# A top-2 routing kernel with uneven token tiles, a zero-filled output tile and a one-input mask

## The chip, the cores and the metric

The kernel runs on one core of one Trainium2 chip. The metric is the device time of one execution in microseconds (us). The kernel before took 14.62 us (median of 3 runs, 14.59 to 14.70). At this length a tenth of a microsecond is 0.7% of an execution.

## The reference

```python
router_logits = np.random.randn(16, 1024, 8).astype(np.float32)     # batch, seq, experts; k = 2

def reference(router_logits, k):
    logits_max = np.max(router_logits, axis=-1, keepdims=True)
    probs = np.exp(router_logits - logits_max)
    probs = probs / np.sum(probs, axis=-1, keepdims=True)
    return np.argsort(probs, axis=-1)[..., -k:]                      # int64: runner-up, winner
```

The softmax keeps the order of the logits, so the task is: for each of 16,384 tokens, the positions of the second largest and the largest of 8 numbers. The output is int64, so each answer is a 32-bit word followed by a zero word.

## The kernel before

The tokens lie on 128 partitions, 128 tokens each, and go through in two tiles of 64. All arithmetic is on VectorE. A first instruction, the pack, overwrites the lowest three bits of each logit with its expert number. Then a tournament of maxima and minima finds the two largest numbers, and the last instruction keeps only the lowest three bits of each.

```python
    andmask = const_pool.tile([P, 1], i32)
    nc.vector.memset(andmask, -8)
    mask4 = const_pool.tile([P, 4], i32)              # 7, 0, 7, 0
    nc.vector.memset(mask4[:, 0::2], 7)
    nc.vector.memset(mask4[:, 1::2], 0)
    for it in range(n_tiles):                         # two tiles of T = 64 tokens
        nc.sync.dma_start(out=x, in_=in_h[:, c0 : c0 + T, :])
        # the pack: x = (x & -8) | expert number, 8 words per token
        nc.vector.scalar_tensor_tensor(out=x_i, in0=x_i, scalar=andmask[:, 0:1], in1=iota_b,
                                       op0=Alu.bitwise_and, op1=Alu.bitwise_or)
        # A = max, Bm = min of experts 0-3 with 4-7 (4 words per token each)
        # T1 = max, UV[0:2] = min of A's halves; UV[2:4] = max of Bm's halves (2 each)
        nc.vector.tensor_reduce(out=FS[:, :, 1], in_=T1, axis=X, op=Alu.max)    # the winner
        nc.vector.tensor_reduce(out=U2, in_=T1, axis=X, op=Alu.min)
        nc.vector.tensor_reduce(out=W, in_=UV, axis=X, op=Alu.max)
        nc.vector.tensor_tensor(out=FS[:, :, 0], in0=U2, in1=W, op=Alu.max)     # the runner-up
        # the mask: 4 words per token, from FS with each word read twice, and 7, 0, 7, 0
        nc.vector.tensor_tensor(out=o_v, in0=fs_b, in1=m4_b, op=Alu.bitwise_and)
        nc.scalar.dma_start(out=out_h[:, c0 : c0 + T, :], in_=o)
```

(The tournament is told in comments.)

Of the kernel before, what the change touches and what calls it, by code (L numbers as in the profile page):

```python
# [1 line left out]

# [4 lines left out]

TOKENS_PER_TILE = 64
USE_POOL_L1 = False  # L10


@with_exitstack
def kernel(
    ctx: ExitStack,
    tc: tile.TileContext,
    router_logits: bass.AP,
    k: bass.AP,
    out: bass.AP,
):  # L20
    nc = tc.nc
    P = nc.NUM_PARTITIONS
    Alu = mybir.AluOpType

    assert isinstance(k, int) and k == 2, f"kernel specialized for k=2, got {k}"

    B, S, E = router_logits.shape
    n_tokens = B * S
    assert E == 8
    assert n_tokens % P == 0  # L30
    T_ALL = n_tokens // P

    fp32 = mybir.dt.float32
    i32 = mybir.dt.int32

    in_h = router_logits.tensor.reshape([P, T_ALL, E])
    out_h = out.tensor.reshape([P, T_ALL, 2]).bitcast(i32)

    const_pool = ctx.enter_context(tc.tile_pool(name="consts", bufs=1))
    x_pool = ctx.enter_context(tc.tile_pool(name="x", bufs=2))  # L40
    mid_pool = ctx.enter_context(tc.tile_pool(name="mid", bufs=2))
    out_pool = ctx.enter_context(tc.tile_pool(name="o", bufs=2))

    iota8 = const_pool.tile([P, E], i32)
    nc.gpsimd.iota(iota8, pattern=[[1, E]], base=0, channel_multiplier=0)  # L45

    andmask = const_pool.tile([P, 1], i32)
    nc.vector.memset(andmask, -8)  # L48

    mask4 = const_pool.tile([P, 4], i32)  # L50
    nc.vector.memset(mask4[:, 0::2], 7)  # L51
    nc.vector.memset(mask4[:, 1::2], 0)  # L52

    T = TOKENS_PER_TILE
    n_tiles = T_ALL // T

    for it in range(n_tiles):
        c0 = it * T

        x = x_pool.tile([P, T, E], fp32)  # L60
        nc.sync.dma_start(out=x, in_=in_h[:, c0 : c0 + T, :])

        x_i = x.bitcast(i32)
        iota_b = iota8[:, None, :].to_broadcast([P, T, E])

        nc.vector.scalar_tensor_tensor(  # L66
            out=x_i,
            in0=x_i,
            scalar=andmask[:, 0:1],
            in1=iota_b,  # L70
            op0=Alu.bitwise_and,
            op1=Alu.bitwise_or,
        )

        A = mid_pool.tile([P, T, 4], fp32)
        Bm = mid_pool.tile([P, T, 4], fp32)
        l1_eng = nc.gpsimd if USE_POOL_L1 else nc.vector
        l1_eng.tensor_tensor(out=A, in0=x[:, :, 0:4], in1=x[:, :, 4:8], op=Alu.max)  # L78
        l1_eng.tensor_tensor(out=Bm, in0=x[:, :, 0:4], in1=x[:, :, 4:8], op=Alu.min)  # L79

        T1 = mid_pool.tile([P, T, 2], fp32)
        UV = mid_pool.tile([P, T, 4], fp32)
        nc.vector.tensor_tensor(out=T1, in0=A[:, :, 0:2], in1=A[:, :, 2:4], op=Alu.max)  # L83
        nc.vector.tensor_tensor(  # L84
            out=UV[:, :, 0:2], in0=A[:, :, 0:2], in1=A[:, :, 2:4], op=Alu.min
        )
        nc.vector.tensor_tensor(  # L87
            out=UV[:, :, 2:4], in0=Bm[:, :, 0:2], in1=Bm[:, :, 2:4], op=Alu.max
        )

        FS = mid_pool.tile([P, T, 2], fp32)
        U2 = mid_pool.tile([P, T], fp32)
        W = mid_pool.tile([P, T], fp32)
        nc.vector.tensor_reduce(  # L94
            out=FS[:, :, 1], in_=T1, axis=mybir.AxisListType.X, op=Alu.max
        )
        nc.vector.tensor_reduce(out=U2, in_=T1, axis=mybir.AxisListType.X, op=Alu.min)  # L97
        nc.vector.tensor_reduce(out=W, in_=UV, axis=mybir.AxisListType.X, op=Alu.max)  # L98
        nc.vector.tensor_tensor(out=FS[:, :, 0], in0=U2, in1=W, op=Alu.max)  # L99

        o = out_pool.tile([P, T, 4], i32)
        o_v = o.rearrange("p t (c two) -> p t c two", two=2)
        fs_b = FS.bitcast(i32)[:, :, :, None].to_broadcast([P, T, 2, 2])
        m4_b = (
            mask4[:, None, 0:4]
            .rearrange("p t (c two) -> p t c two", two=2)
            .to_broadcast([P, T, 2, 2])
        )
        nc.vector.tensor_tensor(out=o_v, in0=fs_b, in1=m4_b, op=Alu.bitwise_and)  # L109

        nc.scalar.dma_start(out=out_h[:, c0 : c0 + T, :], in_=o)


# [1 line left out]
_INS = ['router_logits', 'k']  # L115
_OUTS = [((16, 1024, 2), 'int64')]
#: Inputs that are plain numbers.
_NUMBERS = {'k': 2}


# [26 lines left out]
```

## Time and profile before

| what | value |
|---|---|
| time | 14.62 us (profiled execution 14.69, span 12.9) |
| first input issued, first pack starts | 0.74, 3.75 us |
| VectorE from first pack to end of last mask | 6.59 us (3.75 to 10.34) |
| last store, issue to landing | about 1.8 us |

The first view is the profile's chain of waits: the work that ended last, followed backwards, as shares of the span by engine.

```profile
DVE 51%; DMA 22%; issue 1%; DVEq 0%
```

VectorE (DVE) alone makes up half of the span, the first input transfer another 22%. The rest is the start, before the chain begins, and the last store after the last VectorE instruction. Where that time lies is seen in the timeline. Its columns are: start and length in us, engine, line of the program, operation, output and inputs, shape; in brackets the idle time before and what ended it.

```profile
0.74 0.85 SPq L61 DMA_DIRECT2D x<-in_router_logits_dram  x2
...
3.75 1.41 DVE L66 SCALAR_TENSOR_TENSOR x<-x,andmask,iota 128x512 int32<-128x512 int32 x2 [2.82 <-DMA x<-in_router_logits_dram]
5.08 0.42 DVE L78 TENSOR_TENSOR A<-x 128x256 f32<-128x256 f32 x1
5.42 0.42 DVE L79 TENSOR_TENSOR Bm<-x 128x256 f32<-128x256 f32 x1
5.75 0.28 DVE L83 TENSOR_TENSOR T<-A 128x128 f32<-128x128 f32 x1
...
9.21 0.41 DVE L98 TENSOR_REDUCE W<-UV 128x64 f32<-128x256 f32 x1
9.65 0.23 DVE L99 TENSOR_TENSOR FS<-U,W 128x64 f32<-128x64 f32 x1
9.91 0.43 DVE L109 TENSOR_TENSOR o<-FS,mask 128x256 int32<-128x256 int32 x1
```

Two things are to be read here. Bm starts 0.34 us after A and T 0.33 us after Bm, although A and Bm last 0.42: neighbours overlap, and what an instruction costs is the step from its start to the next start, not its length. And where an instruction needs the result of its neighbour (W, FS and mask at the end) the overlap is lost: FS starts 0.44 us after W, not 0.33.

The DMA issues of the same page give the bytes of one transfer and the median time from issue to landing.

```profile
x<-in_router_logits_dram SPq DMA_DIRECT2D x2, 256.0 KB, 3.0
out_dram<-o ACTq DMA_DIRECT2D x2, 128.0 KB, 1.8
```

### The profile page before, as it was taken

The numbers are of one execution on the slowest core, as the hardware profiler recorded it, in microseconds if no ns is written. First come the engines' busy times: TensorE is split into PE (matmuls) and PEld (weight loads), VectorE is DVE, ScalarE is ACT, GpSimd is POOL, SyncE is SP. The second block draws the span as 40 slices with busy tenths as digits, with TensorE's granted clock in tenths as the row PEclk, the third lists the DMA queues.
The fourth block names the chain that finished last, engine by engine and source line by source line (L and its number), as shares of the span: only waits on it lengthen the run. The fifth ranks groups of instructions, "written<-read, shape, count | busy, mean of one in ns | idle before, by whom it ended". The sixth has DMA issues, their size and how long they took to land.

```text
span 12.9 us, 77 instructions
## 1 busy us (share of the span) xinstructions
DVE 6.6 (51%) x25; POOL 0.3 (3%) x5
## 2 busy tenths in 40 slices
DVE  0030000000039999999999999999988900000000
POOL 2340000000000000000000000000000000000000
DMA  0000048999520000000000000000380000190000
GB/s 0 0 0 0 0 57 222 286 343 406 222 89 0 0 0 0 0 0 0 0 0 0 0 0 0 0 0 0 130 273 3 0 0 0 60 330 16 0 0 0
DMA packets 576, 0.79 MB, mean 61 GB/s; under 512 B 64, under 2 KB 320, under 8 KB 576
## 3 DMA queue, kind: packets, MB, share of 16 engines
q1 hardware_dynamic: 288, 0.52, 12.7%
q10 hardware_dynamic: 288, 0.26, 6.1%
HBM read 0.52 MB, written 0.26 MB: 61 GB/s over the span
## 4 chain that ended last, share of the span: by engine, by line
DVE 51%; DMA 22%; issue 1%; DVEq 0%
DMA x<-in_router_logits_dram 22%; DVE x L66 11%; DVE o L109 6%; DVE Bm L79 5%; DVE A L78 5%; DVE W L98 5%; DVE UV L87 3%; DVE UV L84 3%; DVE T L83 3%; DVE FS L94 3%; DVE U L97 3%; DVE FS L99 3%; DVEq L66 0%
## 5 line engine op out<-in xcount | busy, mean ns | idle before, releaser
L66 DVE SCALAR_TENSOR_TENSOR x<-x,andmask,iota 128x512 int32<-128x512 int32 x2 | 1.4, 748 | 2.8 <-DMA x<-in_router_logits_dram 2.8
L109 DVE TENSOR_TENSOR o<-FS,mask 128x256 int32<-128x256 int32 x2 | 0.8, 422 | 0.0
L79 DVE TENSOR_TENSOR Bm<-x 128x256 f32<-128x256 f32 x2 | 0.8, 419 | 0.0
L78 DVE TENSOR_TENSOR A<-x 128x256 f32<-128x256 f32 x2 | 0.8, 417 | 0.0
L98 DVE TENSOR_REDUCE W<-UV 128x64 f32<-128x256 f32 x2 | 0.8, 408 | 0.0
L84 DVE TENSOR_TENSOR UV<-A 128x128 f32<-128x128 f32 x2 | 0.6, 286 | 0.0
L87 DVE TENSOR_TENSOR UV<-Bm 128x128 f32<-128x128 f32 x2 | 0.6, 286 | 0.0
L83 DVE TENSOR_TENSOR T<-A 128x128 f32<-128x128 f32 x2 | 0.6, 285 | 0.0
L94 DVE TENSOR_REDUCE FS<-T 128x64 f32<-128x128 f32 x2 | 0.6, 279 | 0.0
L97 DVE TENSOR_REDUCE U<-T 128x64 f32<-128x128 f32 x2 | 0.6, 276 | 0.0
L48 DVE MEMSET andmask<- 128x1 int32 x1 | 0.1, 59 | 0.8 <-PEq L128 0.8
L99 DVE TENSOR_TENSOR FS<-U,W 128x64 f32<-128x64 f32 x2 | 0.4, 222 | 0.0
L45 POOL IOTA iota<- 128x8 int32 x1 | 0.1, 135 | 0.4 <-PEq L142 0.4
L128 POOL MEMSET const-float32-0.0<- 128x1 f32 x1 | 0.1, 99 | 0.2 <-issue 0.2
L128 POOL MEMSET const-bfloat16-1.0<- 128x1 bf16 x1 | 0.1, 102 | 0.0
L128 POOL MEMSET const-uint8-127<- 128x1 uint8 x1 | 0.1, 102 | 0.0
L128 POOL MEMSET const-float32-1.0<- 128x1 f32 x1 | 0.1, 99 | 0.0
L51 DVE MEMSET mask<- 128x2 int32 x1 | 0.1, 60 | 0.0
L52 DVE MEMSET mask<- 128x2 int32 x1 | 0.1, 60 | 0.0
## 6 DMA issues: line engine op xcount, KB each, us to landing
x<-in_router_logits_dram SPq DMA_DIRECT2D x2, 256.0 KB, 3.0
out_dram<-o ACTq DMA_DIRECT2D x2, 128.0 KB, 1.8
```

The costliest lines, as they stand in the source:

```text
L66: nc.vector.scalar_tensor_tensor(out=x_i, in0=x_i, scalar=andmask[:, 0:1], in1=iota_b, op0=Alu.bitwise_and, op1=Alu.bitwise_or,)
L78: l1_eng.tensor_tensor(out=A, in0=x[:, :, 0:4], in1=x[:, :, 4:8], op=Alu.max)
L79: l1_eng.tensor_tensor(out=Bm, in0=x[:, :, 0:4], in1=x[:, :, 4:8], op=Alu.min)
L83: nc.vector.tensor_tensor(out=T1, in0=A[:, :, 0:2], in1=A[:, :, 2:4], op=Alu.max)
L84: nc.vector.tensor_tensor(out=UV[:, :, 0:2], in0=A[:, :, 0:2], in1=A[:, :, 2:4], op=Alu.min)
L87: nc.vector.tensor_tensor(out=UV[:, :, 2:4], in0=Bm[:, :, 0:2], in1=Bm[:, :, 2:4], op=Alu.max)
L94: nc.vector.tensor_reduce(out=FS[:, :, 1], in_=T1, axis=mybir.AxisListType.X, op=Alu.max)
L97: nc.vector.tensor_reduce(out=U2, in_=T1, axis=mybir.AxisListType.X, op=Alu.min)
L98: nc.vector.tensor_reduce(out=W, in_=UV, axis=mybir.AxisListType.X, op=Alu.max)
L99: nc.vector.tensor_tensor(out=FS[:, :, 0], in0=U2, in1=W, op=Alu.max)
L109: nc.vector.tensor_tensor(out=o_v, in0=fs_b, in1=m4_b, op=Alu.bitwise_and)
L128: nc = _bacc.Bacc("TRN2", target_bir_lowering=False, num_devices=1)
```

## The change

It wants VectorE to start sooner (a first tile of 32 tokens instead of 64), to keep the smaller tile's work ahead of the second tile's pack (an ordering edge between instructions, which is no wait on a semaphore), and to write half as many words at the end: the zero words are put there by memsets while VectorE waits for its first input, and the mask becomes an instruction with one tensor input. One small constant is also set on GpSimd instead of VectorE, before the first input lands.

```diff
-TOKENS_PER_TILE = 64
+CHUNKS = [32, 96]
...
-    nc.vector.memset(andmask, -8)
-    (mask4: 7, 0, 7, 0)
+    nc.gpsimd.memset(andmask, -8)
+    for it, T in enumerate(CHUNKS):
+        oz = out_pool.tile([P, T, 4], i32, name=f"o{it}", tag=f"o{it}")
+        nc.vector.memset(oz, 0)
+        o_tiles.append(oz)
...
+        if it > 0:
+            tc.add_manual_dep(pack.ins, w_prev.ins.name, ...NoSync...)   # pack behind W of the tile before
...
-        nc.vector.tensor_tensor(out=o_v, in0=fs_b, in1=m4_b, op=Alu.bitwise_and)
+        nc.vector.tensor_scalar(out=o[:, :, 0:4:2], in0=FS.bitcast(i32),
+                                scalar1=7, scalar2=None, op0=Alu.bitwise_and)
```

More of the change, by code (lines that the diff above doesn't have):

```diff
@@ L7 @@
 from concourse._compat import with_exitstack
-TOKENS_PER_TILE = 64
-USE_POOL_L1 = False
+CHUNKS = [32, 96]
+SPLIT_IN_DMA = False
+SPLIT_LAST_OUT = False
+ACT_ZERO_PACK = True
 @with_exitstack
@@ L31 @@
     T_ALL = n_tokens // P
+    assert sum(CHUNKS) == T_ALL
     fp32 = mybir.dt.float32
@@ L47 @@
     andmask = const_pool.tile([P, 1], i32)
-    nc.vector.memset(andmask, -8)
-    mask4 = const_pool.tile([P, 4], i32)
-    nc.vector.memset(mask4[:, 0::2], 7)
-    nc.vector.memset(mask4[:, 1::2], 0)
-    T = TOKENS_PER_TILE
-    n_tiles = T_ALL // T
-    for it in range(n_tiles):
-        c0 = it * T
-        x = x_pool.tile([P, T, E], fp32)
-        nc.sync.dma_start(out=x, in_=in_h[:, c0 : c0 + T, :])
+    nc.gpsimd.memset(andmask, -8)
+    if not ACT_ZERO_PACK:
+        mask4 = const_pool.tile([P, 4], i32)
+        nc.vector.memset(mask4[:, 0::2], 7)
+        nc.vector.memset(mask4[:, 1::2], 0)
+    n_chunks = len(CHUNKS)
+    o_tiles = []
+    for it, T in enumerate(CHUNKS):
+        oz = out_pool.tile([P, T, 4], i32, name=f"o{it}", tag=f"o{it}")
+        nc.vector.memset(oz, 0)
+        o_tiles.append(oz)
+    c0 = 0
+    for it, T in enumerate(CHUNKS):
+        last = it == n_chunks - 1
+        x = x_pool.tile([P, T, E], fp32, name=f"x{it}", tag=f"x{it}")
+        src = in_h[:, c0 : c0 + T, :]
+        if SPLIT_IN_DMA:
+            nc.sync.dma_start(out=x[0:64], in_=src[0:64])
+            nc.scalar.dma_start(out=x[64:128], in_=src[64:128])
+        else:
+            nc.sync.dma_start(out=x, in_=src)
         x_i = x.bitcast(i32)
         iota_b = iota8[:, None, :].to_broadcast([P, T, E])
-        nc.vector.scalar_tensor_tensor(
+        pack = nc.vector.scalar_tensor_tensor(
             out=x_i,
@@ L73 @@
         )
-        A = mid_pool.tile([P, T, 4], fp32)
-        Bm = mid_pool.tile([P, T, 4], fp32)
-        l1_eng = nc.gpsimd if USE_POOL_L1 else nc.vector
-        l1_eng.tensor_tensor(out=A, in0=x[:, :, 0:4], in1=x[:, :, 4:8], op=Alu.max)
-        l1_eng.tensor_tensor(out=Bm, in0=x[:, :, 0:4], in1=x[:, :, 4:8], op=Alu.min)
-        T1 = mid_pool.tile([P, T, 2], fp32)
-        UV = mid_pool.tile([P, T, 4], fp32)
+        if it > 0:
+            tc.add_manual_dep(
+                pack.ins, w_prev.ins.name,
+                mybir.DependencyInfo(
+                    mybir.DependencyClass.NoSync, mybir.DependencyReason.DATA
+                ),
+                reason="work of the chunk before first",
+            )
+        A = mid_pool.tile([P, T, 4], fp32, name=f"A{it}", tag=f"A{it}")
+        Bm = mid_pool.tile([P, T, 4], fp32, name=f"B{it}", tag=f"B{it}")
+        nc.vector.tensor_tensor(out=A, in0=x[:, :, 0:4], in1=x[:, :, 4:8], op=Alu.max)
+        nc.vector.tensor_tensor(out=Bm, in0=x[:, :, 0:4], in1=x[:, :, 4:8], op=Alu.min)
+        T1 = mid_pool.tile([P, T, 2], fp32, name=f"T1{it}", tag=f"T1{it}")
+        UV = mid_pool.tile([P, T, 4], fp32, name=f"UV{it}", tag=f"UV{it}")
         nc.vector.tensor_tensor(out=T1, in0=A[:, :, 0:2], in1=A[:, :, 2:4], op=Alu.max)
@@ L89 @@
         )
-        FS = mid_pool.tile([P, T, 2], fp32)
-        U2 = mid_pool.tile([P, T], fp32)
-        W = mid_pool.tile([P, T], fp32)
+        FS = mid_pool.tile([P, T, 2], fp32, name=f"FS{it}", tag=f"FS{it}")
+        U2 = mid_pool.tile([P, T], fp32, name=f"U2{it}", tag=f"U2{it}")
+        W = mid_pool.tile([P, T], fp32, name=f"W{it}", tag=f"W{it}")
         nc.vector.tensor_reduce(
@@ L97 @@
         nc.vector.tensor_reduce(out=U2, in_=T1, axis=mybir.AxisListType.X, op=Alu.min)
-        nc.vector.tensor_reduce(out=W, in_=UV, axis=mybir.AxisListType.X, op=Alu.max)
+        w_prev = nc.vector.tensor_reduce(out=W, in_=UV, axis=mybir.AxisListType.X, op=Alu.max)
         nc.vector.tensor_tensor(out=FS[:, :, 0], in0=U2, in1=W, op=Alu.max)
-        o = out_pool.tile([P, T, 4], i32)
-        o_v = o.rearrange("p t (c two) -> p t c two", two=2)
-        fs_b = FS.bitcast(i32)[:, :, :, None].to_broadcast([P, T, 2, 2])
-        m4_b = (
-            mask4[:, None, 0:4]
-            .rearrange("p t (c two) -> p t c two", two=2)
-            .to_broadcast([P, T, 2, 2])
-        )
-        nc.vector.tensor_tensor(out=o_v, in0=fs_b, in1=m4_b, op=Alu.bitwise_and)
-        nc.scalar.dma_start(out=out_h[:, c0 : c0 + T, :], in_=o)
+        o = o_tiles[it]
+        if ACT_ZERO_PACK:
+            nc.vector.tensor_scalar(
+                out=o[:, :, 0:4:2],
+                in0=FS.bitcast(i32),
+                scalar1=7,
+                scalar2=None,
+                op0=Alu.bitwise_and,
+            )
+        else:
+            o_v = o.rearrange("p t (c two) -> p t c two", two=2)
+            fs_b = FS.bitcast(i32)[:, :, :, None].to_broadcast([P, T, 2, 2])
+            m4_b = (
+                mask4[:, None, 0:4]
+                .rearrange("p t (c two) -> p t c two", two=2)
+                .to_broadcast([P, T, 2, 2])
+            )
+            nc.vector.tensor_tensor(out=o_v, in0=fs_b, in1=m4_b, op=Alu.bitwise_and)
+        dst = out_h[:, c0 : c0 + T, :]
+        if last and SPLIT_LAST_OUT:
+            nc.scalar.dma_start(out=dst[0:64], in_=o[0:64])
+            nc.sync.dma_start(out=dst[64:128], in_=o[64:128])
+        else:
+            nc.scalar.dma_start(out=dst, in_=o)
+        c0 += T
 _INS = ['router_logits', 'k']
```

## The prediction

> **What bounds the kernel now.** One chain, by the profile's chain of waits: the first input transfer (issued at 0.74 us, released the VectorE at 3.62), then VectorE alone from 3.75 to 10.34 us without a pause, then the last output transfer (issued 10.37, median 1.8 us to landing), then the end of the 12.9 us span. The second input is needed at 4.41 us and is there.
>
> **VectorE's cost per instruction.** From the timeline's start-to-start steps: tensor_tensor on 256 elements per partition 0.33 us, on 128 elements 0.20, on 64 elements 0.13. That is about 0.067 us plus 1.04 ns per element; the two-operation pack (512) steps 0.66, so about 0.13 us fixed. An instruction that needs the result of the one just before it loses another 0.11 to 0.13 us (W at 9.21, then FS at 9.65 instead of 9.54, then mask at 9.91 instead of 9.78).
>
> **What changes.**
> - First tile 32 tokens instead of 64: 128 KB instead of 256. The DMA queue shares give about 90 ns per input packet (2 KB) and 44 ns per output packet (1 KB); a 1 KB input packet I estimate at 50 to 60 ns. Eight packets per engine make it 0.3 us earlier (0.2 to 0.4): the pack starts near 3.45 us. On the critical path in full. The fixed part of the transfer, the larger, stays.
> - Output: the masking tensor_tensor writes 4 words per token; the tensor_scalar writes 2, the zero words come from memsets. That saves 256 elements, 0.27 us, all critical. If the op runs two elements per cycle, another 0.1 us. The Trainium skill, "VectorE: DVE Perf Modes", section "The perf-mode tier table", gives tensor_scalar on 4-byte SBUF data that double rate; no instruction of this trace shows it, so I count it half.
> - The memsets of both output tiles (128 and 384 elements, together at most about 0.7 us) run between 0.8 and 1.6 us, while VectorE waits for data: free.
> - The instruction count after the first landing stays 22.
> - The ordering edge puts the second pack behind W of the first chunk. So pack and A of the first chunk now stand next to each other: +0.11 us. I expect the second pack, then A, to fill the gaps around FS and mask of the first chunk, as A and Bm do now. The second pack starts near 5.2 us, when its input (near 4.3) has long landed.
> - Last store 192 KB instead of 128: 8 packets per engine, half as large again, +0.15 us.
>
> **Sum.** VectorE ends near 9.75 us instead of 10.34 (0.3 landing, 0.32 output, 0.11 back, rest rounding); minus 0.15 for the store: 0.42 us gained. Predicted 14.2 us (ratio 0.97), range 13.95 to 14.42. Chances: faster by over 2% 0.73, within 2% 0.26, slower 0.01.
>
> **What would show it.** First pack starting at 3.35 to 3.55 us; no wait for the second input; tensor_scalar 96 tokens lasting 0.25 us (double rate) or 0.35 (single); memsets over by 1.7 us; last mask ending 9.6 to 9.9; last store 1.9 to 2.0 us to landing.
>
> **What would make it wrong.** The first transfer lands hardly earlier, because its time is latency rather than bytes (then about 14.5, within 2%); the scheduler leaves FS and mask of the first chunk back to back and A right behind the pack (+0.35 us, no gain beyond 2%); strided writes of the tensor_scalar run slowly; or the store of 1.5 KB rows is quicker than I count, with a double-rate tensor_scalar (then 14.0).

## The result

The changed kernel took 14.09 us (median of 12 runs, 14.01 to 14.45), the kernel before in all its runs up to then 14.71 us (15 runs, 14.45 to 14.83). The ratio is 0.964 (95% interval 0.960 to 0.968): faster. Ratios here are the mean time of one kernel's fast runs over that of the other's in the same rounds, so they are not quite the ratio of the medians. On one core "fast" and "slow" only mean that a run lies within 1.5% of the fastest of its kernel or above that. Both profiled executions, 14.69 us before and 14.29 us after, were slow, so the two profiles compare slow with slow.

The timeline of the changed kernel, same columns:

```profile
0.73 0.84 SPq L74 DMA_DIRECT2D x<-in_router_logits_dram  x2
...
0.83 0.57 DVE L62 MEMSET o<- 128x128 int32 x2 [0.83 <-PEq L164]
...
3.45 0.48 DVE L79 SCALAR_TENSOR_TENSOR x<-x,andmask,iota 128x256 int32<-128x256 int32 x1 [2.05 <-DMA x<-in_router_logits_dram]
3.97 0.29 DVE L98 TENSOR_TENSOR A<-x 128x128 f32<-128x128 f32 x1
...
5.04 0.28 DVE L118 TENSOR_REDUCE W<-UV 128x32 f32<-128x128 f32 x1
5.23 1.01 DVE L79 SCALAR_TENSOR_TENSOR x<-x,andmask,iota 128x768 int32<-128x768 int32 x1
6.16 0.19 DVE L119 TENSOR_TENSOR FS<-U,W 128x32 f32<-128x32 f32 x1
6.28 0.56 DVE L98 TENSOR_TENSOR A<-x 128x384 f32<-128x384 f32 x1
6.75 0.19 DVE L123 TENSOR_SCALAR o<-FS 128x64 int32<-128x64 int32 x1
...
9.23 0.26 DVE L119 TENSOR_TENSOR FS<-U,W 128x96 f32<-128x96 f32 x1
9.52 0.26 DVE L123 TENSOR_SCALAR o<-FS 128x192 int32<-128x192 int32 x1
```

The first pack starts 0.30 us sooner. The memsets end at 1.40 us, two microseconds before they could hurt. The first tile's pack and A are now neighbours, and A waits for the pack's end. The second pack and A of the second tile fill the gaps around FS and mask of the first. The last mask lasts 0.26 us where it lasted 0.43. VectorE ends at 9.78 us, 0.56 us sooner, after a stretch of 6.33 us.

And its DMA issues:

```profile
x<-in_router_logits_dram SPq DMA_DIRECT2D x1, 384.0 KB, 3.1
out_dram<-o ACTq DMA_DIRECT2D x1, 192.0 KB, 1.9
x<-in_router_logits_dram SPq DMA_DIRECT2D x1, 128.0 KB, 2.6
out_dram<-o ACTq DMA_DIRECT2D x1, 64.0 KB, 1.6
```

The last store gives back part of it: 192 KB land 1.9 us after their issue, 128 KB took about 1.8. From the end of the last mask to the end of the execution it is 4.51 us, where it was 4.35. From profile to profile 0.40 us remain (14.69 to 14.29).

### The profile page after: what moved, and what is told of

Its sections match the earlier page's. It is cut to its first block, busy times and chain, and to the rows that moved or that the text cites. A ratio compares the mean times of both kernels' runs of the same rounds, so it can differ in the third digit from the quotient of the medians.

```text
span 12.5 us, 77 instructions
## 1 busy us (share of the span) xinstructions
DVE 6.8 (54%) x24; POOL 0.4 (3%) x6
## 4 chain that ended last, share of the span: by engine, by line
DVE 50%; DMA 21%; issue 2%; DVEq 0%
DMA x<-in_router_logits_dram 21%; DVE x L79 11%; DVE A L98 6%; DVE B L99 5%; DVE W L118 5%; DVE UV L104 3%; DVE T L103 3%; DVE UV L107 3%; DVE FS L114 3%; DVE U L117 3%; DVE o L123 3%; DVE FS L119 3%; DVEq L79 0%
## 5 line engine op out<-in xcount | busy, mean ns | idle before, releaser
L79 DVE SCALAR_TENSOR_TENSOR x<-x,andmask,iota 128x256 int32<-128x256 int32 (+1 forms) x2 | 1.5, 747 | 2.0 <-DMA x<-in_router_logits_dram 2.0
L62 DVE MEMSET o<- 128x128 int32 (+1 forms) x2 | 0.5, 272 | 0.9 <-PEq L164 0.8
L98 DVE TENSOR_TENSOR A<-x 128x128 f32<-128x128 f32 (+1 forms) x2 | 0.8, 424 | 0.0
L99 DVE TENSOR_TENSOR B<-x 128x128 f32<-128x128 f32 (+1 forms) x2 | 0.8, 416 | 0.0
L118 DVE TENSOR_REDUCE W<-UV 128x32 f32<-128x128 f32 (+1 forms) x2 | 0.8, 408 | 0.0
L104 DVE TENSOR_TENSOR UV<-A 128x64 f32<-128x64 f32 (+1 forms) x2 | 0.6, 285 | 0.0
L107 DVE TENSOR_TENSOR UV<-B 128x64 f32<-128x64 f32 (+1 forms) x2 | 0.6, 285 | 0.0
L103 DVE TENSOR_TENSOR T<-A 128x64 f32<-128x64 f32 (+1 forms) x2 | 0.6, 284 | 0.0
L114 DVE TENSOR_REDUCE FS<-T 128x32 f32<-128x64 f32 (+1 forms) x2 | 0.6, 278 | 0.0
L117 DVE TENSOR_REDUCE U<-T 128x32 f32<-128x64 f32 (+1 forms) x2 | 0.6, 276 | 0.0
```

What stands on the lines that cost most here:

```text
L62: nc.vector.memset(oz, 0)
L79: pack = nc.vector.scalar_tensor_tensor(out=x_i, in0=x_i, scalar=andmask[:, 0:1], in1=iota_b, op0=Alu.bitwise_and, op1=Alu.bitwise_or,)
L98: nc.vector.tensor_tensor(out=A, in0=x[:, :, 0:4], in1=x[:, :, 4:8], op=Alu.max)
L99: nc.vector.tensor_tensor(out=Bm, in0=x[:, :, 0:4], in1=x[:, :, 4:8], op=Alu.min)
L103: nc.vector.tensor_tensor(out=T1, in0=A[:, :, 0:2], in1=A[:, :, 2:4], op=Alu.max)
L104: nc.vector.tensor_tensor(out=UV[:, :, 0:2], in0=A[:, :, 0:2], in1=A[:, :, 2:4], op=Alu.min)
```

## The experiments

Theory: the gain comes from the output step; the early start is real but is paid back by the gap behind the first pack and by the larger last store. Rival: the early start carries the gain.

The executions of one kernel vary by some 0.3 us, which is as much as the parts to be told apart. All profiles show where that lies: in the start of the first pack. So each profiled execution is split into the start of the first pack and the rest (its time minus that start):

| kernel | profiled time | first pack starts | rest |
|---|---|---|---|
| before | 14.69 | 3.75 | 10.94 |
| before, again (e11) | 14.80 | 3.86 | 10.94 |
| changed | 14.29 | 3.45 | 10.84 |
| changed, again (e5) | 14.27 | 3.43 | 10.84 |
| changed, again (e12) | 14.21 | 3.37 | 10.84 |
| e1 output step only | 14.32 | 3.79 | 10.53 |
| e2 split and edge only | 14.40 | 3.16 | 11.24 |
| e3 changed, no edge | 14.71 | 3.46 | 11.25 |
| e4 changed, two-input mask | 14.16 | 3.19 | 10.97 |
| e6 changed, tiles 16 and 112 | 14.02 | 2.77 | 11.25 |
| e7 changed, last store split | 14.89 | 3.42 | 11.47 |
| e8, e10 losers | 13.47 | 3.18 | 10.29 |
| e9 losers, tiles 24 and 104 | 13.36 | 3.00 | 10.36 |

The rest repeats to 0.01 us in every kernel that was profiled more than once. Below, an execution is called late or early by this start: with a first transfer of 128 KB, late is near 3.45 us and early near 3.17. Within one kernel the profiled starts differ by 0.11 us at most, so it is not shown directly that the rest is the same early and late. What speaks for it: the time from the end of the last mask to the end of the execution is 4.50 to 4.52 us in every profile with a 192 KB store that is not split, early (e2, e4, e8, e10) or late (changed, e3, e5, e12). In e3 and e6 the rest also holds a wait for the second input, so there it depends on when the first pack started.

### e1: the output step on the even tiles

```diff
-CHUNKS = [32, 96]
+CHUNKS = [64, 64]
-        if it > 0:        # the ordering edge
+        if False:
```

> The new output step and zero memsets on the old even tiles (64 and 64 tokens), without the ordering edge. Ledger theory (the split earns 0.3 us at the start and pays 0.11 us for the gap between pack and A and 0.15 us for the larger last store, so it is nearly a wash, and the output step earns 0.35 us): the first pack starts at 3.75 us as before, the last mask ends near 9.97 us, the store lands 1.8 us after issue, and the time is within 0.1 us of the changed kernel, ratio to the kernel before about 0.97. Rival (the earlier start carries the gain): the time stays within 0.1 us of the kernel before.

Measured: 14.09 us (median of 7), ratio 0.963 (0.955 to 0.970), as fast as the whole change. The first pack and the last mask:

```profile
3.79 1.41 DVE L79 SCALAR_TENSOR_TENSOR x<-x,andmask,iota 128x512 int32<-128x512 int32 x2 [2.39 <-DMA x<-in_router_logits_dram]
...
9.75 0.23 DVE L123 TENSOR_SCALAR o<-FS 128x128 int32<-128x128 int32 x1
```

The first pack starts at 3.79 us, as before, and the rest falls from 10.94 to 10.53. The output step alone earns 0.41 us. That the early start alone carries the gain, the rival, is ruled out.

### e2: the split and the edge with the old mask

```diff
-ACT_ZERO_PACK = True
+ACT_ZERO_PACK = False      # tensor_tensor with mask4, 4 words per token
-        nc.vector.memset(oz, 0)
```

> The uneven split and the ordering edge with the old masking operation (four words per token, tile of constants, no zero memsets). Ledger theory: first pack at 3.45 us, last mask ends 0.35 to 0.4 us later than in the changed kernel (near 10.15 us), store 1.9 us, so the time is within 0.1 us of the kernel before, ratio 0.99 to 1.0. Rival (the earlier start carries the gain): ratio about 0.97 or below.

Measured: 14.48 us (6 runs), ratio 0.990 (0.985 to 0.996). The first pack and the last mask:

```profile
3.16 0.49 DVE L78 SCALAR_TENSOR_TENSOR x<-x,andmask,iota 128x256 int32<-128x256 int32 x1 [2.27 <-DMA x<-in_router_logits_dram]
...
9.34 0.56 DVE L137 TENSOR_TENSOR o<-FS,mask 128x384 int32<-128x384 int32 x1
```

The rest grows from 10.94 to 11.24 us: 0.15 us in VectorE's stretch (6.74 us) and the remainder behind it, in the larger store. Against that stands the earlier start, 0.30 us between executions that land late. Late against late, the two sum to nothing. All six runs of e2 were near 14.47 us and its profile starts the pack at 3.16 us; the split's 1% here comes with such early landings (more on them under "Why the prediction was right"), and in e11 one kernel against itself differs by as much. The parts add up: 10.94 - 0.41 + 0.30 = 10.83, and the changed kernel has 10.84.

### e3: the changed kernel without the edge

```diff
-        if it > 0:
+        if False:
```

> The changed kernel without the ordering edge: the compiled order then has the second pack right behind the first. Theory that the edge is needed by the split: the second pack waits for the second input until about 4.35 us, VectorE is idle some 0.45 us from 3.9 us on, and against that pack and A no longer wait for each other (0.11 us), so the kernel is about 0.35 us slower than the changed kernel and about as slow as the kernel before. Rival (the edge is an ornament): the same time as the changed kernel within 0.1 us.

Measured: 14.64 us (6 runs), ratio 0.994 (0.986 to 1.003): as slow as the kernel before. Its timeline shows why:

```profile
3.46 0.49 DVE L79 SCALAR_TENSOR_TENSOR x<-x,andmask,iota 128x256 int32<-128x256 int32 x1 [2.06 <-DMA x<-in_router_logits_dram]
4.40 1.02 DVE L79 SCALAR_TENSOR_TENSOR x<-x,andmask,iota 128x768 int32<-128x768 int32 x1 [0.46 <-DMA x<-in_router_logits_dram]
5.34 0.28 DVE L98 TENSOR_TENSOR A<-x 128x128 f32<-128x128 f32 x1
```

Without the edge the second pack is queued right behind the first, and VectorE idles 0.46 us for the second input with the first tile's whole tournament ready to run. The rest is 0.41 us longer than with the edge. With even tiles (e1) this order costs nothing: both packs follow each other in 1.41 us without a pause, as before. The split needs the edge.

### e4: two words per token, but two tensor inputs

```diff
+    seven = const_pool.tile([P, 2], i32)
+    nc.vector.memset(seven, 7)
...
-            nc.vector.tensor_scalar(out=o[:, :, 0:4:2], in0=FS.bitcast(i32), scalar1=7, ...)
+            nc.vector.tensor_tensor(out=o[:, :, 0:4:2], in0=FS.bitcast(i32),
+                in1=seven[:, None, :].to_broadcast([P, T, 2]), op=Alu.bitwise_and)
```

> The changed kernel with the masking of two words per token done by a tensor_tensor against a tile of sevens, same output pattern and element count. If the tensor_scalar runs at double rate, this operation on 192 elements lasts 0.35 us instead of 0.26, and the kernel is 0.1 us slower (in the profile: last mask ends 0.1 us later). If the short duration comes from something else (fewer words, the strided write), it lasts 0.26 us here as well and the time is the same.

Measured: 14.22 us (6 runs), ratio 0.972 (0.967 to 0.978). The two masks in the timeline of e4:

```profile
6.49 0.22 DVE L125 TENSOR_TENSOR o<-FS,seven 128x64 int32<-128x64 int32 x1
...
9.29 0.36 DVE L125 TENSOR_TENSOR o<-FS,seven 128x192 int32<-128x192 int32 x1
```

The same 192 words with the same output pattern last 0.36 us with two tensor inputs and 0.26 with one. From 64 to 192 words the length grows by 0.14 us with two inputs (0.22 to 0.36) and by 0.07 with one (0.19 to 0.26), so the rate itself is double. The rest grows by 0.13 us. So of the output step's 0.41 us about 0.13 is the rate of the one-input form and about 0.28 the halved number of words.

### e5: the changed kernel again

No edit.

> The changed kernel once more, unedited, as the yardstick for the runs beside it and to see the two groups of times (near 14.03 and near 14.32 us) again. Theory: the groups differ only in when the first input transfer lands (2.3 against 2.6 us after its issue, as the profiles of the split-only and two-word kernels against that of the changed kernel suggest). A profile that falls in the fast group then shows the first pack at about 3.17 us and the same 6.33 us from the start of the first pack to the end of the last mask. Rival: the groups differ in VectorE's work or in the last store.

Measured: 14.08 us (6 runs, 14.02 to 14.27), ratio 0.959 (0.955 to 0.963). The profile fell on the slowest run: first pack at 3.43 us, VectorE's stretch again 6.33 us (to 9.76 us). An early execution of this very kernel was not caught here. Kernels with the same first transfer that were caught early (e2, e4, e8, e10) start at 3.16 to 3.19 us.

### e6: tiles of 16 and 112 tokens

```diff
-CHUNKS = [32, 96]
+CHUNKS = [16, 112]
```

> The changed kernel with tiles of 16 and 112 tokens. If the landing time still falls with the bytes of the first tile (0.3 us for each halving of 128 KB would be too much; 4 packets-worth of 0.06 us per engine less give 0.15 to 0.2 us at half the row length), the first pack starts 0.1 to 0.2 us earlier, VectorE's stretch from first pack to last mask stays at 6.33 us, the last store takes 0.04 us more, and the kernel is about 0.1 us faster. If the landing is at its latency floor at 128 KB, nothing is gained and the time is the same or slightly more.

Measured: 14.02 us (6 runs, 13.99 to 14.06), ratio 0.956 (0.953 to 0.959). Its timeline:

```profile
2.77 0.35 DVE L79 SCALAR_TENSOR_TENSOR x<-x,andmask,iota 128x128 int32<-128x128 int32 x1 [1.37 <-DMA x<-in_router_logits_dram]
...
4.36 1.15 DVE L79 SCALAR_TENSOR_TENSOR x<-x,andmask,iota 128x896 int32<-128x896 int32 x1 [0.23 <-DMA x<-in_router_logits_dram]
```

The landing moved more than either theory had it: the first pack starts 0.4 us sooner than even in the early executions with 128 KB (3.16 to 3.19 us). But now the first tile is too short to reach the second input, and VectorE idles 0.23 us for it. The six times also lie within 0.07 us. That would fit a kernel that is held by the second landing, whatever the first one does, but it is not shown: in e8, which never waits for the second input, five of six times lie within 0.02 us. A smaller first tile helps only as far as its work fills the time to the second landing.

### e7: the last store on two queues

```diff
-SPLIT_LAST_OUT = False
+SPLIT_LAST_OUT = True      # partitions 0-63 from ScalarE's queue, 64-127 from SyncE's
```

> The changed kernel with its last store issued as two halves of 64 partitions, from the scalar and the sync engine. If the 0.85 us between issue and first byte grow with the number of rows that one issue has to describe, the store lands 0.1 to 0.2 us sooner and the kernel gains as much. If the time is the fixed latency plus the bytes, which are the same on the same engines, the time stays within 0.05 us.

Measured: 14.67 us (6 runs), ratio 1.002 (0.996 to 1.008). Neither expectation held: it lost 0.6 us against the changed kernel beside it (14.08). Its last stores in the timeline, and then the page's DMA issues for them:

```profile
9.78 0.53 SPq L143 DMA_DIRECT2D out_dram<-o  x1
9.79 0.55 ACTq L142 DMA_DIRECT2D out_dram<-o  x1
```

```profile
out_dram<-o SPq DMA_DIRECT2D x1, 96.0 KB, 2.2
out_dram<-o ACTq DMA_DIRECT2D x1, 96.0 KB, 2.4
```

Each issue now takes 0.53 to 0.55 us, where the unsplit stores of the changed kernel took 0.34 and 0.37, and half the bytes land in 2.2 and 2.4 us instead of 1.9. The Trainium skill, "DMA: Bandwidth & Descriptors", section "Issuing engines are not separate DMA queues", says that issuing from several engines "will only save the time on the sequencer"; here it did not even save that. Whether the two queues or the half-height transfers did it, this run does not tell apart.

### e8: the runner-up as one maximum over the losers

The runner-up is the largest of those that lost a comparison: four in the first round, two in the second, one in the last. They are written side by side into one tile and reduced at once. The last round compares two columns instead of reducing over two words.

```diff
-        # Bm, UV (2), FS (2), U2, W: 7 instructions, all of the tournament but A and T1
+        nc.vector.tensor_tensor(out=L[:, :, 0:4], in0=x[:, :, 0:4], in1=x[:, :, 4:8], op=Alu.min)
+        nc.vector.tensor_tensor(out=L[:, :, 4:6], in0=A[:, :, 0:2], in1=A[:, :, 2:4], op=Alu.min)
+        nc.vector.tensor_tensor(out=L[:, :, 6], in0=T1[:, :, 0], in1=T1[:, :, 1], op=Alu.min)
+        nc.vector.tensor_tensor(out=FS[:, :, 1], in0=T1[:, :, 0], in1=T1[:, :, 1], op=Alu.max)
+        w_prev = nc.vector.tensor_reduce(out=FS[:, :, 0], in_=L[:, :, 0:7], axis=X, op=Alu.max)
```

> A candidate to beat both: same tiles, edge and output step, but the runner-up is found as one maximum over the seven losers of the tournament (4, 2 and 1 of the three rounds), and the two final comparisons are tensor_tensor on one word per token instead of reduces over two. Per token 30 elements instead of 32, 9 instructions per tile instead of 11, and one dependent pair fewer at the end. By the cost per instruction (0.067 us plus 1.04 ns per element, 0.11 us per dependent neighbour): 0.27 plus 0.27 plus 0.11, so 0.6 to 0.65 us less from first pack to last mask (5.7 us instead of 6.33), time about 13.4 us in the fast group, ratio to the kernel before about 0.92. If instructions do not cost a fixed amount each, only 0.27 us.

Measured: 13.47 us (6 runs), ratio 0.918 (0.915 to 0.921), correct. The end of its timeline:

```profile
7.46 0.33 DVE L110 TENSOR_TENSOR L<-T 128x96 f32<-128x96 f32 x1
7.63 0.25 DVE L113 TENSOR_TENSOR FS<-T 128x96 f32<-128x96 f32 x1
7.82 0.85 DVE L116 TENSOR_REDUCE FS<-L 128x96 f32<-128x672 f32 x1
8.71 0.26 DVE L122 TENSOR_SCALAR o<-FS 128x192 int32<-128x192 int32 x1
```

VectorE's stretch is 5.79 us instead of 6.33, so 0.54 us less where 0.6 to 0.65 were expected. That is twice what the saved elements alone give (0.27), so the fixed cost per instruction and the lost dependent neighbour count. A piece of the shortfall is visible: the write of one word into rows of eight lasts 0.33 us, the same count into rows of two 0.25, and the reduce starts only after its end. By the prediction's cost per instruction that delays the reduce by an estimated 0.02 us here and 0.04 in the first tile.

### e9 and e10: the losers with tiles of 24 and 104, and again with 32 and 96

```diff
-CHUNKS = [32, 96]
+CHUNKS = [24, 104]
```

> The losers kernel with tiles of 24 and 104 tokens. The run with tiles of 16 and 112 showed the first pack at 2.77 us but the second pack idle until the second input at 4.36 us, and the losers kernel with 32 and 96 starts its second pack at 4.94 us, 0.58 us after that input is due. So there is room for an earlier start. Expected: first pack near 3.0 us, second pack near 4.5 us with no wait or one under 0.1 us, last mask ends 0.15 to 0.2 us sooner than with 32 and 96, last store 0.03 us longer, time about 13.33 us. Rival: the first landing moves in a step and not with the bytes (64 KB and 128 KB differ by 0.4 us or more), so 96 KB lands as late as 128 KB and nothing is gained (13.47 us).

> The losers kernel with 32 and 96 tokens once more, unedited, as the yardstick beside the run with 24 and 104: 13.47 us, with single executions near 13.7 us where the first input lands late.

Measured beside each other, on another chip than e1 to e8: 13.35 us for 24 and 104 (6 runs, 13.33 to 13.36), ratio 0.925 (0.922 to 0.928), and 13.47 for 32 and 96 (5 runs), ratio 0.933 (0.931 to 0.936). The packs of e9:

```profile
3.00 0.42 DVE L79 SCALAR_TENSOR_TENSOR x<-x,andmask,iota 128x192 int32<-128x192 int32 x1 [1.60 <-DMA x<-in_router_logits_dram]
...
4.52 1.08 DVE L79 SCALAR_TENSOR_TENSOR x<-x,andmask,iota 128x832 int32<-128x832 int32 x1
```

The earlier start came as expected and the second pack waits for nothing. This is the fastest version, correct, and beats both kernels; between 24 and 32 tokens the split is worth 0.12 us. The kernel before took 14.42 us (14.70 in e8), so these ratios are not to be compared with the 0.918 of e8.

### e11 and e12: both kernels again, side by side

No edits.

> The kernel before, unedited, to get a second profile of it and its groups of times beside the changed kernel's. Its executions centred on 14.7 us in three calls and on 14.42 us in the last call, which ran on another chip. Theory: that is the same difference of the first input's landing that splits the changed kernel's times (0.28 us). A profile at about 14.4 us shows the first pack at about 3.47 us instead of 3.75 and the same 6.59 us to the end of the last mask; one at about 14.7 us shows the first pack at 3.75 us. Rival: VectorE's stretch or the store differs.

> The changed kernel beside it. Theory: compared within one group of landing times (late with late, early with early), the change is worth 0.38 to 0.42 us, a ratio of about 0.973, not the 0.96 that the fast executions of one against the mixed or late ones of the other gave. Where this call lands early as a whole, the ratio comes out near 0.973. Rival: the ratio stays at 0.96 in every state, so that the change earns more than the profiles show.

Measured: the kernel before 14.71 us (6 runs, 14.63 to 14.82), beside the runs of this same kernel for comparison (the yardstick) at 14.60 (11 runs, 14.40 to 14.77). That is a ratio of 1.015 (1.008 to 1.023) of a kernel to itself, so the intervals of this document do not cover how groups of runs of one kernel differ, and a ratio within 1.5% of 1 tells nothing by itself. The changed kernel took 14.09 us (6 runs, 14.02 to 14.25), ratio 0.970 (0.963 to 0.977) to the yardstick; both verdicts of this call are "unclear". Its mean over that of the 6 runs of e11 is 14.115 / 14.718 = 0.959. Their profiles are in the table: the rest is 10.94 and 10.84 us again. So the theory that executions of one kernel differ only in the first landing holds as far as these starts reach (3.75 to 3.86 us before, 3.37 to 3.45 changed). It fails in another point: I had expected groups of times, and 3.37 us in e12 lies between the early and the late starts, so the landing is not two-valued. The ratio of 0.973 that I expected between equal landings was not measured either, since no early execution of the kernel before was caught in a profile.

## Why the prediction was right

The forecast was 14.2 us, ratio 0.97, and 14.09 us and 0.964 were measured. Point by point:

- First pack near 3.45 us: 3.45 in the profile, 0.30 us sooner. 128 KB landed in 2.6 us in late executions and in 2.3 to 2.4 in early ones. The sum behind this number (half-size packets at 50 to 60 ns) is not confirmed: the same sum gave 0.15 to 0.2 us for the step to 64 KB, and e6 moved by 0.4 or more. That it came out at 0.30 here may be luck.
- Output step: 0.27 us for the words and, half counted, 0.1 for a double rate. The double rate is there: 0.26 us for 192 words, against 0.36 in e4. The whole step earned 0.41 us (e1), 0.09 more than the 0.32 that was counted, because the double rate was counted half. The Trainium skill, "VectorE: DVE Perf Modes", section "The perf-mode tier table", has this rate for tensor_scalar on fp32 in SBUF; the trace agrees for int32 with a bitwise operation and a strided output.
- Gap of 0.11 us between the first pack and A: it is in the timeline (A starts 0.04 us after the pack's end instead of overlapping it), and the order of the other instructions was as foreseen. VectorE's stretch grew by 0.15 us in e2.
- Last store +0.15 us, landing in 1.9 to 2.0 us: 1.9. The rest grew by 0.30 us in e2, of which 0.15 is not VectorE's.
- End of the last mask 9.6 to 9.9 us: 9.78.

Two points were weaker than the total. The prediction did not add up its own terms of the split (-0.30, +0.11, +0.15), which sum to -0.04, so it never said that the uneven tiles earn nothing between equally late landings; e1 and e2 show it. And it took the ordering edge for a cost of 0.11 us, where e3 shows that without it the change earns nothing (0.41 us).

The median came out 0.11 us below the forecast, and against the kernel before's later median of 14.71 us the gain is 0.62. Profile against profile, both late, the gain is 0.40 us, and 0.42 was predicted. The rest looks like landing, which the prediction did not foresee: 7 of the 12 executions of the changed kernel lie at 14.10 us or less and 5 at 14.29 or more, as an earlier landing by some 0.28 us would place them, whereas most of the kernel before's lay near 14.7.

All recorded runs say more. Take each run's time minus the rest of its kernel as an estimate of its first start (without e3 and e6, whose rest holds a wait). The earliest start is 3.16 us with a first transfer of 128 KB (53 runs) and 3.44 with 256 KB (72 runs), so 0.28 us apart, like the late profiles. But the medians, 3.20 and 3.71, are 0.51 apart: 42 of the 53 lie within 0.15 us of their earliest start, and only 23 of the 72. By this estimate the split, which costs 0.30 us of rest, is worth about 0.2 us in a typical run, though nothing between equal landings, which fits e2 (14.48 against 14.64) and the 0.62 us (0.41 of it the output step). It is not settled: e1, with 256 KB, was early in four of its seven runs, and on the chip of e9 and e10 nearly all runs of both sizes were early. Why a landing is early or late, and whether the smaller first transfer makes it early more often, stays open. The kernel before was also seen near 14.4 us.

## What to carry to other kernels

Split a first tile off only after adding up what it costs at the other end: the larger last store, the neighbours that no longer overlap, and the wait for the second input, which needs the first tile's work to be ahead in the queue and long enough. Words that never change can be written while the engine waits for its first data, and an instruction with one tensor input instead of two may then run at twice the rate (192 words in 0.26 us against 0.36). In an execution of 14 us, subtract the varying first landing before comparing versions: the rest repeated to 0.01 us where the times spread by 0.3. Then look at the landing by itself, over many runs: a smaller first transfer may be worth more, or less, than one profile of each kernel says.

## What the Trainium skill lacked or had wrong

- "VectorE: DVE Perf Modes", section "The TRN2 errata", gives `58 + FD/Accel` cycles and says that the measured fixed term is about 150. Both are in this trace, for different things: a tensor_tensor on 256 words lasts 0.42 us (0.267 us of words at 0.96 GHz and 0.15 us), but the next one starts after 0.33 to 0.34 (0.067 us, 64 cycles). The section does not say that the first is the length and the second the step. "Perfetto Trace Analysis", section "Optimizing Scalar/DVE Operations", does: about 60 ns of engine time per instruction, and about twice that in the profiled duration; here it was 67 and 150 ns.
- The tier table of "VectorE: DVE Perf Modes" does not name int32 or bitwise operations; the page's section "What auto-detection actually checks" sets no type for the two-port double rate. Here 192 words took 0.26 us as tensor_scalar and 0.36 as tensor_tensor, both into every second word.
- "DMA: Bandwidth & Descriptors", section "Latency and other measured facts", gives about 0.6 us to the first byte for transfers issued from SyncE and ScalarE. It does not say from where it counts. In the changed kernel the first input was issued at 0.73 us and its bytes begin to show at 1.70 us, in slices of 0.05 us; the last store was issued at 9.82 us and its bytes show from 10.65 us on. So it was 0.8 to 1.0 us from the start of the issuing instruction and 0.5 to 0.6 from its end (it lasts 0.36 and 0.34 us).
- The same page, section "Anatomy of one DMA — SWDGE (gpsimd) path", has one fixed cost of about 2.0 us per transfer, for transfers issued from GpSimd. Stores issued from ScalarE landed after 1.5 us (32 KB), 1.6 (64 KB), 1.7 to 1.8 (128 KB), 1.9 (192 KB) and 2.0 (224 KB); first loads issued from SyncE after 1.9 us (64 KB), 2.2 (96 KB), 2.3 to 2.6 (128 KB) and 2.9 to 3.0 (256 KB).
- The same page, "Rules for kernel authors", advises against two transfers to disjoint partition halves because they serialize; it has no figure for what they can cost: 0.6 us in e7.
- I found no page that mentions that the landing of one and the same first transfer varies by 0.3 us from execution to execution (first pack at 3.16 to 3.46 us for 128 KB, over several kernels with the same first transfer).
